# A two-layer decoder on one core: the opening of the chained gated MLP in another engine order

## The chip, the core and the metric

The kernel runs on one core of one Trainium2 chip. The metric is the device time of one execution in microseconds (us), and lower is better. The kernel before takes 1467.89 us, the median of 3 runs (1467.75 to 1471.22).

The engines are named as the profile names them: PE is the matrix engine (PEld its weight loads), DVE the vector engine, ACT the scalar engine, POOL the general engine, which here only issues accumulating transfers, and SP the engine that issues the loads. Each engine takes its instructions in the order of its queue.

## The reference

Two layers over 512 tokens of width 1024, all in float32. Each layer is a token mixer, a cross-attention into 256 memory tokens, and a gated MLP; what concerns the change is the end of the attention and the MLP:

```
def cross_attn(x, mem, norm, mem_norm, wq, wk, wv, wo):
    ...
    s = jnp.einsum('bqhd,bkhd->bhqk', q, k).astype(jnp.float32) * (XA_HD ** -0.5)
    p = jax.nn.softmax(s, axis=-1).astype(x.dtype)
    o = jnp.einsum('bhqk,bkhd->bqhd', p, v).reshape(Bn, S, D_MODEL)
    return o @ wo

def conv_ffn(x, norm, w_up, dw_w, dw_b, w_down):
    h = rms_norm(x, norm) @ w_up
    g = causal_dwconv(h[..., :D_FF], dw_w, dw_b)
    u = h[..., D_FF:]
    return (jax.nn.gelu(g) * u) @ w_down

def reference(...):
    for layer in range(DEPTH):
        ...
        x = x + cross_attn(x, mem, ...)
        x = x + conv_ffn(x, f_norm[layer], f_w_up[layer], ...)
    return rms_norm(x, final_norm)
```

D_FF is 3072, so the MLP has 24 chunks of 128 channels on the gate side and 24 on the value side; the convolution has width 3 and runs along the tokens.

## The kernel before

**Number format.** Every float32 operand of a product is split in two: `high` copies it with ACT into the matrix format, `low` subtracts that copy from the original with DVE. A product of 128 x 128 by 128 x 512 is then three matmuls (`mm3`, L184: high by high, high by low, low by high). So each weight piece costs a load (SP), an ACT copy, a DVE subtraction and PE time.

**The MLP's units.** The first two of the 24 chunks (PLAIN = 2) are computed plainly, in `opening` (L991): four products of 24 matmuls each, `start(0)` to `start(3)` (gate 0, value 0, gate 1, value 1), with weight pieces called w0 to w3 here, each loaded into one of three `raw` buffers. The other 22 chunks are computed in pairs of gate and value by a scheme of seven block products instead of eight (`unit`, L925): the weight pair of a chunk is held as four blocks, and sums of blocks are needed too. The two input sums of the scheme are made by `Seven.sums` (L742) from the token activations, four calls, the last of them in the opening.

**The blocks of a weight pair** (`Blocks`, L777). `load` brings two blocks into a `raw` buffer (r and z), `load_second` brings a12 and a22 into two of four `wa` buffers. The sums are made in place by accumulating transfers that POOL issues, one after the other, inside `low`: after a11 is split, r += z; after a22, z += a22; after s3, r += a22; after s2, r += a12. So the blocks a11, s3, s2, s4 are the same buffer r at four times, s1 is z after its transfer, and `high("s3")` has to wait until r += z has landed. `wa` buffers become free when s3 (a22) and s2 (a12) are done.

The first pair, chunk 2, is called the first pair below (`first` in the code, `up` in the attention), chunk 3 the second (`second`).

**The order.** In the units of the attention and in the whole MLP the order of PE, ACT, DVE and POOL is the program's (`tc.manual_schedule(engines=ORDERED)`); SP's loads are ordered by a planner at build time. The end of the attention (L695 to L724) is not written out: there the planner orders all engines from its own estimates of durations, in which a piece that is traced earlier has priority among those that it takes to be ready. This end consists of the output products `back(n, ks)` (24 matmuls for each of eight n), the scores and softmax of the last head (`scores(3)`: PE, then DVE L501 to L505, the exponentials on ACT L510, DVE L515, the scaling on ACT L517), its transposes on PE (L531), the split of these (`turned(3)`), its product with the values (`mixed(3)`), the splits of the first pair's blocks a11, a22, a12, s3 and s1 (`prepare`), and three of the four calls of `sums`.

**The opening before.** PE runs start(0), the mean of squares for the norm (L287, L288), start(1), start(2), start(3), then a11 of the first pair (`ahead`, L918). ACT copies that result into a second bank (L922); after that PE can add s2 to the second bank, having done s1 in a third. ACT and DVE meanwhile make the root and the reciprocal of the norm (L306, L308), the splits of w2 and w3, the gate chains of chunks 0 and 1 (L1008 scale, L889 first tap, L892 two more taps, L894 gelu, L1011), the products with the values (L1014, L1016, L1019), the fourth `sums`, and the splits s2 of the first pair and a11 and a22 of the second. L922 is traced last of all of these on ACT.

ACT holds one set of function tables at a time; a load of another set shows as ACT_TABLE_LOAD before the first function that needs it. Copies, squares and the linear taps run with whichever set is there.

Of the kernel before, what the change touches and what calls it, by code (L numbers as in the profile page):

```python
# [10 lines left out]
F32 = mybir.dt.float32  # L11
F32R = mybir.dt.float32r
AF = mybir.ActivationFunctionType
# [48 lines left out]
def trunk(ctx: ExitStack, tc: tile.TileContext, I: dict, out: list):  # L62
# [407 lines left out]
    def attention(layer, norm, mem, nxt, six, up):  # L470
# [17 lines left out]
        def score(h, half):  # L488
            ps = aux_ps()
            for j in range(2):  # L490
                qc = 2 * half + j
                for d in range(2):
                    c = 2 * h + d
                    mm3(
                        ps[:, j * M : (j + 1) * M], blk(q[c], qc * P),
                        mem.key(c), d == 0, d == 1,
                    )
            mx = small.tile([P, 2], F32, tag="mx", name=nm("mx"))
            e = tmp_f()
            both = e.rearrange("p (a b) -> p a b", a=2)  # L500
            V.tensor_tensor(  # L501
                both, ps.rearrange("p (a b) -> p a b", a=2), Memory.r.unsqueeze(1).broadcast_to([P, 2, M]), op=ALU.mult
            )
            V.tensor_reduce(mx, both, axis=mybir.AxisListType.X, op=ALU.max)
            V.tensor_tensor(mx, mx, rq[:, 2 * half : 2 * half + 2], op=ALU.mult)  # L505
            yield
            sm = small.tile([P, 2], F32, tag="sm", name=nm("sm"))
            for j in range(2):
                qc = 4 + 2 * half + j
                A.activation(  # L510
                    e[:, j * M : (j + 1) * M], e[:, j * M : (j + 1) * M], AF.Exp,
                    bias=mx[:, j : j + 1], scale=rq[:, qc : qc + 1], accum_out=sm[:, j : j + 1],
                )
            yield
            V.reciprocal(sm, sm)  # L515
            for j in range(2):
                A.activation(e[:, j * M : (j + 1) * M], e[:, j * M : (j + 1) * M], AF.Copy, scale=sm[:, j : j + 1])  # L517
            es.setdefault(h, []).append(e)
            yield

        def scores(h):
            for half in range(2):
                for _ in score(h, half):
                    pass
# [20 lines left out]
        def mixed(h):  # L545
            for d, out in enumerate(mix(h)):
                o[2 * h + d] = split(out)
# [154 lines left out]

        back(0, range(4))
        mixed(2)
        scores(3)
        back(0, range(4, 6))
        back(4, range(6))
        prepare("a11")
        transpose(3)
        turned(3)  # L710
        back(1, range(6))
        prepare("a22")
        mixed(3)
        prepare("a12", "s3")
        seven = Seven(nxt)
        for k in range(4):
            for n in (k, k + 4):
                back(n, range(6 if n in acc else 0, C))
            if k == 1:
                prepare("s1")  # L720
            if k < 3:
                for _ in seven.sums(k):
                    pass
# [53 lines left out]
    class Blocks:  # L777
# [8 lines left out]
            self.r, self.z = raw[:, :T], raw[:, T:]  # L786

        def load_second(self):
            self.a12, self.a22 = [tmp.tile([P, T + 4], F32, tag="h", name=nm("wa"), bufs=4)[:, :T] for _ in range(2)]
            nc.sync.dma_start(self.a12, self.src[:, D + T :])  # L790
            nc.sync.dma_start(self.a22, self.src[:, D : D + T])

        def high(self, name):
            if self.ring:
# [38 lines left out]
    def ffn(layer, norm, nxt, seven, pairs):  # L833
# [91 lines left out]
        def unit(c):  # L925

            nonlocal left, chains
            G, F = chains
            down, seeded = downs.get(c), c > GC
            H = main_ps()[:, :M]  # L930
            m(c, H, "s1", seven.T1)
            high(c + 1, "s3")
            next(left, None)
            low(c + 1, "s3")

            m(c, F, "s2", seven.T2, False)
            next(left, None)
            u, f, g = tmp_f(), tmp_f(), tmp_f()
            A.activation(u[:, :M], F, AF.Copy)
            next(left, None)  # L940
            high(c + 1, "a22")

            m(c, G, "a12", seven.B21, False)
            next(left, None)
            if down:
                d = [down.bank(i, seeded) for i in range(2)]
            next(left, None)
            low(c + 1, "a22")
            times_r(g, G, left_half)
            high(c, "s4")  # L950

            m(c, F, "s3", seven.T3, False)
            A.activation(u[:, M:], F, AF.Copy)
            low(c, "s4")
            add(f[:, right_half], H, u[:, M:])
            V.tensor_tensor(f[:, right_half], f[:, right_half], norm.r[:, right_half], op=ALU.mult)
            high(c + 2, "a11")
            low(c + 2, "a11")
            high(c + 1, "a12")
            low(c + 1, "a12")  # L960
            if down:
                for ks in (range(GC - 1), (GC - 1,)):
                    for i in range(2):
                        down.products(i, d[i], seeded, ks)
            if c + 3 in pairs:
                pairs[c + 3].load()
            if c + 2 in pairs:
                pairs[c + 2].load_second()
            if c >= GC - 1 and c + 1 in downs:
                downs[c + 1].w.high()  # L970
                downs[c + 1].w.low()
            if c + 2 in downs and c + 2 <= CF:
                downs[c + 2].load()
            high(c + 1, "s1")
            low(c + 1, "s1")
            high(c + 1, "s2")
            low(c + 1, "s2")
            if down:
                down.home(0, d[0], seeded)

            if c + 1 in pairs:
                chains = ahead(c + 1)
            if down:
                down.home(1, d[1], seeded)

            m(c, H, "s4", seven.B22, False)
            m(c, F, "a22", seven.T4, False)
            left = gating(c, g, f, u, F, H)
            next(left)

        def opening():  # L991

            nonlocal left, chains
            ps, y = {}, {}

            def start(i):
                ps[i] = main_ps()
                x = w.pop(0)
                for k in range(C):
                    mm3(ps[i], blk(x, k * P), norm.x[k], k == 0, k == C - 1)  # L1000

            def fetch(i):
                w.append(Piece(I["wup"][(layer * 2 + i % 2) * PLAIN + i // 2]))
                w[-1].high()

            def gate(c):
                g = tmp_f()
                V.tensor_tensor(g, ps.pop(2 * c), norm.r, op=ALU.mult)  # L1008
                for y[c] in gate_conv(c, g):
                    yield  # L1010
                V.tensor_tensor(y[c], y[c], norm.r, op=ALU.mult)  # L1011

            def values(c):
                V.tensor_tensor(y[c], ps.pop(2 * c + 1), y[c], op=ALU.mult)  # L1014
                ys[c] = act_r(), act_r()
                A.activation(ys[c][0], y[c], AF.Copy)  # L1016

            def close(c):
                V.tensor_tensor(ys[c][1], y[c], ys[c][0].bitcast(F32), op=ALU.subtract)  # L1019

            def both(c, name):
                high(c, name)
                low(c, name)

            ss = split(norm.ss)
            start(0)
            fetch(2)
            w[-1].low()
            norm.r = scale_of(mean_of(ss))
            Norm.due = None  # L1030

            start(1)
            fetch(3)
            w[-1].low()
            g = gate(0)
            next(g)
            both(first, "s2")
            next(g)
            next(g)
            pairs[second].load()  # L1040
            pairs[second].load_second()
            downs[GC].load()
            t = seven.sums(3)
            next(t)
            next(g, None)

            start(2)
            next(t, None)
            values(0)
            both(second, "a11")  # L1050
            close(0)

            start(3)
            g = gate(1)
            next(g)
            both(second, "a22")
            next(g)
            next(g)
            pairs[second + 1].load()
            next(g, None)  # L1060
            chains = ahead(first)

            def rest():
                values(1)
                yield
                close(1)

            left = rest()

        left, chains = None, None  # L1070
        first, second = PLAIN, PLAIN + 1
        done.update((first, name) for name in ("a11", "a22", "a12", "s3", "s1"))
        with tc.high_priority(AHEAD):
            w = [Piece(I["wup"][(layer * 2 + k) * PLAIN]) for k in range(2)]
            for x in w:
# [803 lines left out]
```

## Time and profile before

| | |
|---|---|
| median of 3 runs | 1467.89 us (1467.75 to 1471.22) |
| profiled execution, its own time | 1468.71 us |
| its span, first to last instruction | 1466.9 us |
| granted PE clock, mean of the span | 0.989 |
| PEld, DVE, ACT, POOL busy | 87%, 74%, 62%, 22% of the span |

The profile is one execution. A row of a timeline gives the start, the duration, the engine, the line of the kernel, the operation, output<-inputs with the shape, the count of merged instructions, and in brackets the idle time before it with what released it. Matmuls overlap: at full clock a 128x512 matmul is listed with 0.39 us but starts 0.23 us after the one before, and a 128x256 one with 0.28 us starts 0.12 us after. Time on PE is therefore best read from start to start. The two layers are two separate passes through the code: layer 0's attention ends and its MLP opens between about 300 and 420 us, layer 1's between about 1005 and 1125 us.

### The profile page before, as it was taken

The page shows a single profiled execution, that of the slowest core. Times are in us where ns is not written, and L with a number is a line of the kernel's source. Part 1 is how long each engine was busy: PE and PEld are TensorE (multiplying, and loading weights), DVE is VectorE, ACT ScalarE, POOL GpSimd, SP SyncE. Part 2 cuts the span into 40 slices and gives each one's busy share as a digit, 9 for nine tenths or more (in the row PEclk, how much of TensorE's full clock was granted, in tenths as well). Part 3 has the DMA queues.
Part 4 walks back from the last instruction along what each step waited for, and adds up shares of the span by engine and source line. Part 5 has one row for each costly group of instructions (what it writes and reads, how often), then busy time and mean ns, then how long its engine had stood idle before and what let it go on. Part 6 is the DMA issues. An engine that isn't in the chain of part 4 may idle for free.

```text
span 1466.9 us, 22867 instructions
## 1 busy us (share of the span) xinstructions
PE 1430.8 (98%) x8650; PEld 1270.4 (87%) x8650; DVE 1079.3 (74%) x1796; ACT 905.0 (62%) x1588; POOL 317.7 (22%) x333
## 2 busy tenths in 40 slices
PE   9999999999899999999999999998989999999998
PEld 7988888978799999999988777897868999999997
DVE  6987775858677666676789997877767676676665
ACT  7678755657456666566665558676555565666664
POOL 0012300200122222222008991011002222222211
PEclk9999999999999999999999999999999999999999
DMA  8522333543477777677442364255237777777651
GB/s 294 192 86 87 98 117 80 118 106 101 112 172 189 163 166 181 161 166 173 130 129 86 116 181 150 79 113 122 89 94 164 172 167 183 164 174 178 154 135 58
DMA packets 80319, 205.37 MB, mean 140 GB/s; under 512 B 9040, under 2 KB 9552, under 8 KB 80208
## 3 DMA queue, kind: packets, MB, share of 16 engines
q1 hardware_dynamic: 51120, 151.20, 33.6%
q0 software_dynamic: 28800, 52.44, 20.3%
q8 instruction: 67, 1.10, 0.3%
q14 instruction: 44, 0.36, 0.1%
q10 hardware_dynamic: 288, 0.27, 0.1%
HBM read 146.21 MB, written 2.10 MB: 101 GB/s over the span
## 4 chain that ended last, share of the span: by engine, by line
PE 81%; DVE 6%; DMA 5%; ACT 3%; issue 3%; POOL 2%; SPq 0%; POOLq 0%; ACTq 0%; DVEq 0%
PE mm L186 19%; PE mm L187 19%; PE mm L188 19%; PE aux L186 7%; PE aux L187 7%; PE aux L188 7%; PE mm L458 2%; DMA raw<-wa 2%; DMA raw<-raw 1%; DMA raw<-in_wv 1%; DVE bigr L817 1%; POOL actf L1480 1%; ACT tmp L510 1%; DVE tmp L892 1%; DVE wlo L167 0%
## 5 line engine op out<-in xcount | busy, mean ns | idle before, releaser
L187 PE MATMUL mm<-act,whi 128*128 128x512 f32 (+2 forms) x1061 | 370.7, 349 | 0.5 <-DVE act L181 0.4
L186 PE MATMUL mm<-act,whi 128*128 128x512 f32 (+2 forms) x1061 | 370.7, 350 | 0.0
L188 PE MATMUL mm<-act,wlo 128*128 128x512 f32 (+2 forms) x1061 | 370.3, 349 | 0.0
L187 PEld LDWEIGHTS mm<-act,whi 128*128 128x128 f32 x1061 | 201.9, 190 | 27.8 <-DVE act L167 1.0
L186 PEld LDWEIGHTS mm<-act,whi 128*128 128x128 f32 x1061 | 202.0, 191 | 27.6 <-ACT tmp L1479 0.8
L188 PEld LDWEIGHTS mm<-act,wlo 128*128 128x128 f32 x1061 | 201.8, 190 | 25.3 <-DVE wlo L167 0.6
L186 PE MATMUL mm<-bigr,bigr 128*128 128x256 f32 x704 | 202.0, 287 | 16.4 <-ACT mm L922 11.9
L188 PE MATMUL mm<-bigr,bigr 128*128 128x256 f32 x704 | 201.1, 286 | 0.4 <-DVE bigr L817 0.4
L187 PE MATMUL mm<-bigr,bigr 128*128 128x256 f32 x704 | 200.9, 285 | 0.0
L810 ACT ACTIVATE bigr<-raw 128x512 fp32r<-128x512 f32 x176 | 105.4, 621 | 109.1 <-DMA raw<-wa 97.2
L817 DVE TENSOR_TENSOR bigr<-raw,bigr 128x512 fp32r<-128x512 f32 x176 | 117.6, 688 | 70.5 <-ACT bigr L810 70.5
L186 PE MATMUL aux<-act,whi 128*128 128x512 f32 x399 | 155.9, 391 | 0.0
L187 PE MATMUL aux<-act,whi 128*128 128x512 f32 x399 | 155.7, 390 | 0.0
L188 PE MATMUL aux<-act,wlo 128*128 128x512 f32 x399 | 155.2, 389 | 0.0
L186 PEld LDWEIGHTS mm<-bigr,bigr 128*128 128x128 f32 x704 | 136.8, 194 | 18.0 <-ACT mm L922 12.3
L166 ACT ACTIVATE whi<-raw 128x1024 fp32r<-128x1024 f32 (+1 forms) x95 | 96.5, 1020 | 85.8 <-PE mm L187 46.2
L188 PEld LDWEIGHTS mm<-bigr,bigr 128*128 128x128 f32 x704 | 136.9, 194 | 0.9 <-DVE bigr L817 0.9
L187 PEld LDWEIGHTS mm<-bigr,bigr 128*128 128x128 f32 x704 | 137.0, 195 | 0.0
L820 POOL DMA_DIRECT2D raw<-raw x50 | 43.2, 864 | 329.9 <-DVE wlo L817 193.0
L828 POOL DMA_DIRECT2D raw<-wa x50 | 43.1, 862 | 299.6 <-DVE bigr L817 211.7
L167 DVE TENSOR_TENSOR wlo<-raw,whi 128x1024 fp32r<-128x1024 f32 (+1 forms) x75 | 90.3, 1209 | 22.3 <-ACT whi L166 22.0
L171 DVE TENSOR_TENSOR tmp<-mm,tmp 128x256 f32<-128x256 f32 x130 | 53.9, 419 | 65.8 <-PE mm L188 64.1
(353 smaller groups left out, 3126.4 us busy)
## 6 DMA issues: line engine op xcount, KB each, us to landing
raw<-wa POOLq DMA_DIRECT2D x150, 256.0 KB, 5.3
wa<-in_wpair SPq DMA_DIRECT2D x88, 256.0 KB, 3.3
raw<-in_wpair SPq DMA_DIRECT2D x44, 512.0 KB, 4.8
big<-in_wdown SPq DMA_DIRECT2D x44, 512.0 KB, 4.2
raw<-raw POOLq DMA_DIRECT2D x50, 256.0 KB, 4.8
raw<-in_pw SPq DMA_DIRECT2D x24, 512.0 KB, 3.3
raw<-in_win SPq DMA_DIRECT2D x20, 512.0 KB, 3.3
raw<-in_wk SPq DMA_DIRECT2D x16, 512.0 KB, 3.7
```

The lines of the kernel that those rows point to most:

```text
L166: A.activation(hi, src, AF.Copy)
L167: fetched[1] = (eng or V).tensor_tensor(lo, src, hi.bitcast(F32), op=ALU.subtract)
L171: V.tensor_tensor(out, a, b, op=ALU.add)
L186: PE.matmul(ps, wh, xh, start=first, stop=False, skip_group_check=onto)
L187: PE.matmul(ps, wh, xl, start=False, stop=False, skip_group_check=onto)
L188: PE.matmul(ps, wl, xh, start=False, stop=last, skip_group_check=onto)
L458: PE.matmul(p, m[j], x, start=k == 0 and j == 0 and x is hi, stop=k == C - 1 and x is lo)
L510: A.activation(e[:, j * M : (j + 1) * M], e[:, j * M : (j + 1) * M], AF.Exp, bias=mx[:, j : j + 1], scale=rq[:, qc : qc + 1], accum_out=sm ...
L810: A.activation(self.w[name][0], self.block(name), AF.Copy)
L817: V.tensor_tensor(lo, self.block(name), hi.bitcast(F32), op=ALU.subtract)
L820: G.dma_start(self.r, self.z, accum_op=ALU.add)
L828: G.dma_start(self.r, self.a12, accum_op=ALU.add)
```

## The change

In the attention's last head:

```diff
             for j in range(2):
-                A.activation(e[:, j * M : (j + 1) * M], e[:, j * M : (j + 1) * M], AF.Copy, scale=sm[:, j : j + 1])
+                part = e[:, j * M : (j + 1) * M]
+                score.last = A.activation(part, part, AF.Copy, scale=sm[:, j : j + 1]).ins
...
         mixed(2)
+        prepare("a11", "a22")
         scores(3)
         back(0, range(4, 6))
         back(4, range(6))
-        prepare("a11")
         transpose(3)
         turned(3)
         back(1, range(6))
-        prepare("a22")
+        with tc.issue_after(score.last):
+            A.activation(small.tile([P, 1], F32, tag="warm", name=nm("root"), bufs=1), eps, AF.Sqrt)
+            prepare("a12", "s3")
         mixed(3)
-        prepare("a12", "s3")
...
-            if k == 1:
-                prepare("s1")
+            if k in (1, 2):
+                prepare("s%d" % k)
```

`issue_after` queues ACT's instructions of the block behind the last scaling of the softmax, in order of issue only. The tiny square root makes the table load happen there. s2 of the first pair is now split here, at k = 2, and no longer in the opening.

In the loads of a pair, a22 comes before a12; in the first unit the load of the pair after next moves to the opening:

```diff
-            self.a12, self.a22 = [...]
-            nc.sync.dma_start(self.a12, self.src[:, D + T :])
+            self.a22, self.a12 = [...]
             nc.sync.dma_start(self.a22, self.src[:, D : D + T])
+            nc.sync.dma_start(self.a12, self.src[:, D + T :])
...
-            if c + 2 in pairs:
+            if c + 2 in pairs and c > first:
                 pairs[c + 2].load_second()
```

In the opening:

```diff
-            norm.r = scale_of(mean_of(ss))
+            start(1, range(1))
+            mean = mean_of(ss)
             Norm.due = None
-
-            start(1)
+            root = tmp_f()
+            A.activation(root, mean, AF.Sqrt, bias=eps)
+            A.activation(small.tile([P, 1], F32, tag="warm", name=nm("gelu"), bufs=1), eps, AF.Gelu_apprx_tanh)
+            norm.r = small.tile([P, T], F32, tag="r", name=nm("r"), bufs=1)
+            V.reciprocal(norm.r, root)
+            start(1, range(1, C))
+            pairs[second].load()
+            pairs[second].load_second()
             fetch(3)
-            w[-1].low()
             g = gate(0)
             next(g)
-            both(first, "s2")
-            next(g)
-            next(g)
-            pairs[second].load()
-            pairs[second].load_second()
+            w[-1].low()
+            pairs[second + 1].load()
+            pairs[second + 1].load_second()
             downs[GC].load()
-            t = seven.sums(3)
+            t = seven.sums(3, lambda: (next(g), next(g)))
             next(t)
             next(g, None)
 
             start(2)
+            both(second, "a11")
+            values(0)
             next(t, None)
-            values(0)
-            both(second, "a11")
             close(0)
...
             next(g)
             next(g)
-            pairs[second + 1].load()
             next(g, None)
             chains = ahead(first)
...
-        done.update((first, name) for name in ("a11", "a22", "a12", "s3", "s1"))
+        done.update((first, name) for name in ("a11", "a22", "a12", "s3", "s1", "s2"))
```

`start(i, ks)` now takes the range of the eight contraction steps, so the first step of start(1), three matmuls, runs before the mean. The function handed to `sums` is called between its two ACT copies (L747) and its DVE differences (L753 to L759): the second and third tap of gate 0 and its gelu come there.

More of the change, by code (lines that the diff above doesn't have):

```diff
@@ L788, in load_second @@
         def load_second(self):
-            self.a12, self.a22 = [tmp.tile([P, T + 4], F32, tag="h", name=nm("wa"), bufs=4)[:, :T] for _ in range(2)]
+            self.a22, self.a12 = [tmp.tile([P, T + 4], F32, tag="h", name=nm("wa"), bufs=4)[:, :T] for _ in range(2)]
+            nc.sync.dma_start(self.a22, self.src[:, D : D + T])
             nc.sync.dma_start(self.a12, self.src[:, D + T :])
-            nc.sync.dma_start(self.a22, self.src[:, D : D + T])
         def high(self, name):
@@ L994, in opening, with start @@
             ps, y = {}, {}
[L996 to L1000, printed above, removed]
+            def start(i, ks=range(C)):
+                if ks[0] == 0:
+                    ps[i] = main_ps()
+                for k in ks:
+                    mm3(ps[i], blk(w[0], k * P), norm.x[k], k == 0, k == C - 1)
+                if ks[-1] == C - 1:
+                    w.pop(0)
             def fetch(i):
```

## The prediction

> **What bounds the kernel now.** I read the busy times on the page first, then PE's waits, then PE's timeline around each long wait, then the queues of the engine that ended it.
>
> ```profile
> PE 1430.8 (98%) x8650; PEld 1270.4 (87%) x8650; DVE 1079.3 (74%) x1796; ACT 905.0 (62%) x1588; POOL 317.7 (22%) x333
> ...
> PE mm L186 <- ACT mm L922: 11.9, 2, 6.0
> PE aux L531 <- ACT tmp L517: 7.0, 4, 2.9
> PE mm L186 <- ACT bigr L810: 3.0, 2, 1.6
> ```
>
> PE is the bound, so only its holes are worth anything. The change aims at the two largest rows: the copy L922 in the two MLP openings and the softmax of the last head (L517) in the two attention ends. The third stays (below).
>
> The softmax hole, layer 0 and then layer 1, from start to start:
>
> ```profile
> 302.25 1.03 PE L531 MATMUL aux<-ident,tmp 128*128 128x128 f32 x8
> 303.04 0.48 PE L186 MATMUL mm<-act,whi 128*128 128x512 f32 x1
> ...
> 316.69 0.39 PE L188 MATMUL mm<-act,wlo 128*128 128x512 f32 x1
> ...
> 321.04 1.54 PE L531 MATMUL aux<-ident,tmp 128*128 128x128 f32 x6 [0.85 <-ACT tmp L517]
> 322.24 0.78 PE L186 MATMUL mm<-act,whi 128*128 128x512 f32 x1
> 322.81 0.63 PE L187 MATMUL mm<-act,whi 128*128 128x512 f32 x1
> ...
> 326.17 0.40 PE L186 MATMUL mm<-act,whi 128*128 128x512 f32 x1
> ...
> 1021.43 0.39 PE L188 MATMUL mm<-act,wlo 128*128 128x512 f32 x1
> ...
> 1029.38 0.39 PE L187 MATMUL mm<-act,whi 128*128 128x512 f32 x1
> ```
>
> The first two rows give eight transposes at full clock: 0.79 us. From 316.69 to 326.17 are 9.48 us for one 0.23 step, eight transposes and nine 0.23 steps, which need 0.23 + 0.79 + 2.04 = 3.06. So layer 0 loses 6.4 us: the wait itself, and then 0.63 us matmuls at a lower clock. In layer 1, 7.95 us hold one step, eight transposes and four steps (1.93): 6.0 lost.
>
> Why the softmax is late:
>
> ```profile
> 310.86 0.68 DVE L501 TENSOR_TENSOR tmp<-aux,rs 128x512 f32<-128x512 f32 x1
> 315.02 0.69 DVE L817 TENSOR_TENSOR bigr<-raw,bigr 128x512 fp32r<-128x512 f32 x1 [3.48 <-ACT bigr L810]
> 315.63 0.68 DVE L504 TENSOR_REDUCE mx<-tmp 128x2 f32<-128x512 f32 x1
> ...
> 314.35 0.63 ACT L810 ACTIVATE bigr<-raw 128x512 fp32r<-128x512 f32 x1 [4.98 <-DMA raw<-raw]
> ```
>
> The split of s3 stands in both queues in the middle of the softmax and waits for r += z to land. DVE idles 3.48 us for it with the maximum (L504) queued behind.
>
> The openings, layer 0, then layer 1 with its mean:
>
> ```profile
> 386.13 0.28 PE L188 MATMUL mm<-act,wlo 128*128 128x256 f32 x1
> 386.78 0.38 PE L186 MATMUL mm<-bigr,bigr 128*128 128x256 f32 x1 [0.37 <-DVE tmp L1014]
> ...
> 388.19 0.28 PE L188 MATMUL mm<-bigr,bigr 128*128 128x256 f32 x1
> 394.43 0.58 PE L186 MATMUL mm<-bigr,bigr 128*128 128x256 f32 x1 [5.96 <-ACT mm L922]
> ...
> 397.80 0.28 PE L186 MATMUL mm<-act,whi 128*128 128x256 f32 x1
> ...
> 1072.13 0.39 PE L188 MATMUL mm<-act,wlo 128*128 128x512 f32 x1
> 1073.58 0.50 PE L288 MATMUL stat<-act,ones 128*128 128x512 f32 x1 [0.23 <-DVE act L167]
> 1073.92 0.39 PE L186 MATMUL mm<-act,whi 128*128 128x512 f32 x1
> ...
> 1091.59 0.28 PE L188 MATMUL mm<-act,wlo 128*128 128x256 f32 x1
> 1104.45 0.28 PE L186 MATMUL mm<-act,whi 128*128 128x256 f32 x1
> ```
>
> Layer 0: 386.13 to 397.80 is 11.67 us for 28 starts (1 + 11 + 1 + 15), which need 28 x 0.12 = 3.36; lost 8.3. Layer 1: 12.86 us for 34 starts (1 + 11 + 1 + 21; 4.08); lost 8.8. The mean in layer 1: 1.79 us for three 0.23 steps; lost 1.1, because its input comes late. All holes together: 6.4 + 6.0 + 8.3 + 8.8 + 1.1 = 30.6 us. That is the ceiling of this change.
>
> **The change part by part.**
>
> *Softmax.* a12 and s3 go behind the last scaling on ACT, and so behind the softmax on DVE too, since their subtraction needs ACT's copy. L504 then follows L501 at 310.86 + 0.60 = 311.5 instead of 315.63, 4.2 earlier, and the third transpose, which needs the second half, is released at 321.04 - 4.2 = 316.9. PE is free at 316.69 + 0.23 = 316.9. The hole closes, and the lower clock with it: 12.4 us for both layers. s3 loses nothing by coming later: r += z landed at 314.35, before its new turn, and its first reader on PE is in the units, 70 us on.
>
> *New in that place*: a table load and a tiny root on ACT, ahead of `turned(3)`.
>
> ```profile
> 894.00 0.60 ACT L1626 ACTIVATE tmp<-aux 128x512 f32<-128x512 f32 x1 [1.12 <-PE aux L298]
> 894.62 1.28 ACT L1627 ACT_TABLE_LOAD   x1
> 895.91 0.20 ACT L1627 ACTIVATE root<-tmp 128x1 f32<-128x1 f32 x1
> ```
>
> Such a pair took 1.5 us elsewhere. Behind it wait the two copies of `turned(3)`, their subtractions, and `mixed(3)` on PE; ahead of `mixed(3)` PE has `back(1)`, 18 steps of 0.23 = 4.1 us, and the copies and subtractions need some 2 of them (0.63 and 0.69 a piece, as in the rows above, partly side by side). So I cost it at nothing; without that cover it is 1.5 per layer. The Trainium skill (ScalarE: Activation LUTs, What ACT_TABLE_LOAD costs) counts a drain of about 1.38 us besides the 1.28, 2.66 per switch. The rows above show no such gap: the load begins 0.02 us after a busy ACT ends and the next function starts 0.01 us after it. By the page each hold in the tail would be 2.9 us, still about inside the cover, and the two loads that leave the opening's chain would free 5.3 instead of 2.6 us; the sum on PE would hardly move, since PE's holes are the ceiling.
>
> *Opening.* L922 is the end of a chain; here are its parts that change:
>
> ```profile
> 368.72 1.28 ACT L306 ACT_TABLE_LOAD   x1 [0.72 <-PE stat L288]
> 370.02 0.69 ACT L306 ACTIVATE tmp<-stat,eps 128x512 f32<-128x512 f32 x1
> ...
> 374.01 1.16 DVE L203 TENSOR_TENSOR wlo<-raw,whi 128x1024 fp32r<-128x1024 f32 x1
> 375.08 0.68 DVE L1008 TENSOR_TENSOR tmp<-mm,r 128x512 f32<-128x512 f32 x1
> ...
> 377.84 0.75 DVE L892 SCALAR_TENSOR_TENSOR tmp<-tmp,par,tmp 128x511 f32<-128x511 f32 x1
> ...
> 382.63 0.42 DVE L753 TENSOR_TENSOR tmp<-tmp,tmp 128x256 f32<-128x256 f32 x1 [3.26 <-ACT tmp L747]
> ...
> 387.95 0.69 DVE L817 TENSOR_TENSOR wlo<-raw,whi 128x512 fp32r<-128x512 f32 x1 [1.22 <-ACT whi L810]
> ```
>
> (a) The root's table is loaded before: 1.30, but three matmuls of start(1) come ahead of the mean, 0.68 later in layer 0: 0.6 gained. In layer 1 the mean's input is late anyway, so the full 1.3. (b) w3's subtraction no longer stands between reciprocal and L1008: 1.07. (c) L1008 to the taps: 2.76 before, with s2's split between; after, L1008 (0.61) and w3's subtraction (1.14): 1.0 gained. (d) DVE's 3.26 us behind gelu's table load and ACT's two copies go, since the load is done during the reciprocal and the copies during w3's subtraction: 3.3. (e) DVE's 1.22 for a11's copy shrinks to about 0.7, as that copy is queued ahead of L1016: 0.5. Sum: 6.5 in layer 0, 7.2 in layer 1.
>
> What is needed: in layer 0 the hole before 394.43 (6.12 beyond a step) and the one before 386.78 (0.53), 6.65; in layer 1 the same and the mean's 1.11, 7.75. So 0.2 and 0.6 us stay. Holes this short should not lower the clock as 6 us did. What is late next is still L922, with no slack.
>
> *Moved loads.* The second pair's raw load goes ahead of w3's, so w3 gets the buffer that w2 frees:
>
> ```profile
> 345.77 14.21 SPq L195 DMA_DIRECT2D raw<-in_wup  x4
> 369.29 6.24 SPq L785 DMA_DIRECT2D raw<-in_wpair  x2
> ...
> raw<-in_wup SPq DMA_DIRECT2D x4, 512.0 KB, 3.3
> ```
>
> w3 was issued by 360.0 and will be at 369.3, where the second pair's was; with 3.3 us it lands at 372.6, its copy (twice as wide as the 0.63 one above, so about 1.1) ends at 373.7, and L889, queued behind on ACT, has its input about 374.0 (L1008 at 375.08 - 0.6 - 1.07, and 0.6 for itself). Covered by a third of a us. start(3) needs w3 only after start(1) and start(2), 48 steps of 0.23 or 11 us after the mean. a22 before a12, and both earlier, cost nothing: PE has waited on neither. s2's split in the tail adds 0.5 on ACT and 0.6 on DVE at k = 2; start(0)'s 5.4 us and the three moved matmuls hide it; uncovered, up to 0.6 per layer.
>
> *What stays.* The third row of PE's waits, 3.0 us in two, is the stall at s1 of chunk 4. It hangs on POOL's transfers, which start from the first unit's progress; they move with PE, and the units are unchanged.
>
> **Sum.** 30.6 - 0.2 - 0.6 = 29.8. For what the trace of before can't show (the planner's new order in the attention's end, the root's load) I take 1.3 off, between 0 and 3.0 + 1.2 (both covers gone): 28.5. From the profiled execution's 1468.7 that gives 1440.2; the median lies 0.8 below that execution: 1439.4 us.
>
> **The rivals.**
> - *A new wait for w3* (15%). If w3's load takes longer, ACT's copy of it holds back L889 and the whole chain. The cover is thin, and a load at that place shares the DMA engines with the second pair's. Landing 3 us later, plus about 1.5 of low clock as after 394.43, costs 4 per layer: 1447.
> - *The softmax hole stays in part* (10%), because the planner puts another waiting split into the softmax, or s3's ahead of `turned(3)`. For it: it did so before. Against: r += z lands early enough. Half of 12.4 lost: 1446; all: 1452.
> - *The gain is given back at chunk 4* (8%): POOL's transfers take their own time while PE comes 8 us earlier. Against: they start behind L953 of the same unit. 4 per layer: 1447.
> - *Better* (7%): the stall at chunk 4 goes as well (3.0): 1436.
> - *It doesn't do what it says* (2%): the planner's order and L922 stay: 1467.
> - *Slower* (2%): w3's load stands on SP's in-order queue behind a `wa` load that waits for the first pair's s3 or s2. Each us late beyond the cover is paid on both layers; it decides against the change at (28.5 + 4.4) / 2 = 16.5 us. No load here took half of that; 1475.
>
> My forecast has 56%. The range 1435 to 1451 takes it, the better case and nearly all of the first three rivals. About 0.3% (4.4 us) is what a measurement of this kernel can tell from no change: faster 0.95, same 0.03, slower 0.02.
>
> **What would show it.** PE's waits on L922 under 1.5 us in total and on L517 under 1; no 0.63 us matmuls after the last transposes; no table load between the mean and the reciprocal; the wait on s1 (L810) still near 3 us. Wrong would be a wait of ACT on w3's load ahead of L889, or a longer row of PE on L810.

## The result and the profile after

The kernel after takes 1446.2 us, the median of 4 runs (1444.8 to 1447.83), beside 1467.91 us for the kernel before in the same call (4 runs, 1467.75 to 1471.22): a ratio of 0.9847, 95% interval 0.983 to 0.9864, or 21.7 us less. The forecast was 1439.4 us, range 1435 to 1451. The profiled execution of after is its slowest, 1447.83 us (span 1446.0), 20.9 us under the profiled execution of before; the ledger below is made between these two.

First the busy times on the page and the longest of PE's waits (us in total, times, longest):

```profile
PE 1424.8 (99%) x8650; PEld 1264.9 (87%) x8650; DVE 1079.0 (75%) x1796; ACT 906.1 (63%) x1592; POOL 318.2 (22%) x333
...
PE mm L186 <- ACT bigr L812: 4.0, 2, 2.0
PE stat L298 <- DVE actf L1502: 1.7, 1, 1.7
PE mm L186 <- DVE tmp L171: 1.3, 2, 0.7
PE mm L186 <- ACT tmp L941: 1.1, 2, 0.8
PE mm L186 <- ACT whi L801: 1.1, 2, 0.6
PE mm L186 <- ACT mm L924: 1.1, 2, 0.6
```

Lines have moved by one or two: L922 is now L924, L810 is L812, L517 is L518. The copy's wait fell from 11.9 to 1.1 us and the softmax's 7.0 us are gone. But the stall at s1 grew from 3.0 to 4.0, L171 from 0.4 to 1.3, and L801, the weight copies of the last attention unit, is new. L298 lies between the two layers, outside the stretches that the change touches; it was 0.9 in before.

The same stretches of PE as in the prediction, from start to start. The softmax of layer 0 and of layer 1:

```profile
317.92 0.39 PE L188 MATMUL mm<-act,wlo 128*128 128x512 f32 x1
318.15 1.03 PE L532 MATMUL aux<-ident,tmp 128*128 128x128 f32 x8
...
321.08 0.39 PE L186 MATMUL mm<-act,whi 128*128 128x512 f32 x1
...
1012.12 0.39 PE L188 MATMUL mm<-act,wlo 128*128 128x512 f32 x1
1012.35 1.03 PE L532 MATMUL aux<-ident,tmp 128*128 128x128 f32 x8
...
1014.15 0.39 PE L187 MATMUL mm<-act,whi 128*128 128x512 f32 x1
```

The eight transposes stand in one row again, with no idle time and no 0.63 us matmuls behind them. Layer 0 takes 321.08 - 317.92 = 3.16 us where it took 9.48; layer 1 takes 2.03 where it took 7.95.

The openings, then the stall at s1 that ends the first units:

```profile
381.04 0.28 PE L188 MATMUL mm<-act,wlo 128*128 128x256 f32 x1
...
383.32 0.39 PE L186 MATMUL mm<-bigr,bigr 128*128 128x256 f32 x1 [0.56 <-ACT mm L924]
...
385.22 0.28 PE L186 MATMUL mm<-act,whi 128*128 128x256 f32 x1
...
405.79 0.39 PE L186 MATMUL mm<-bigr,bigr 128*128 128x256 f32 x1 [1.94 <-ACT bigr L812]
...
1056.42 0.40 PE L186 MATMUL mm<-act,whi 128*128 128x512 f32 x1
1057.09 0.50 PE L187 MATMUL mm<-act,whi 128*128 128x512 f32 x1 [0.26 <-DVE act L223]
...
1059.14 0.50 PE L288 MATMUL stat<-act,ones 128*128 128x512 f32 x1 [0.22 <-DVE act L167]
1059.48 0.40 PE L186 MATMUL mm<-act,whi 128*128 128x512 f32 x1
...
1076.45 0.28 PE L188 MATMUL mm<-act,wlo 128*128 128x256 f32 x1
...
1078.72 0.39 PE L186 MATMUL mm<-bigr,bigr 128*128 128x256 f32 x1 [0.55 <-ACT mm L924]
...
1081.34 0.28 PE L186 MATMUL mm<-act,whi 128*128 128x256 f32 x1
...
1101.64 0.39 PE L186 MATMUL mm<-bigr,bigr 128*128 128x256 f32 x1 [2.02 <-ACT bigr L812]
```

And the two s1 stalls of before, which the prediction had not shown:

```profile
416.93 0.39 PE L186 MATMUL mm<-bigr,bigr 128*128 128x256 f32 x1 [1.59 <-ACT bigr L810]
...
1122.72 0.39 PE L186 MATMUL mm<-bigr,bigr 128*128 128x256 f32 x1 [1.45 <-ACT bigr L810]
```

PE runs the same 8650 matmuls in nearly the same order, so the two traces can be matched matmul by matmul, and the difference of the starts is what has been gained so far:

| stretch | forecast | measured |
|---|---|---|
| last attention unit, layer 0 / 1 | 0 | -1.4 / -1.1 |
| softmax | +6.4 / +6.0 | +6.3 / +5.9 |
| mean, layer 1 | +1.1 | -0.1 |
| opening, less what was to stay of L922 | +8.1 / +8.2 | +7.5 / +8.0 |
| end of opening to the stall at s1 | 0 | -1.4 / -2.0 |
| all the rest | -1.3 | -0.8 |
| sum | 28.5 | 20.9 |

The openings are 11.67 - (385.22 - 381.04) = 7.5 and 12.86 - (1081.34 - 1076.45) = 8.0. The stretch to s1 took 416.93 - 397.80 = 19.13 us in layer 0 and takes 405.79 - 385.22 = 20.57; in layer 1 it took 1122.72 - 1104.45 = 18.27 and takes 20.30. So the holes that the change aims at closed nearly as forecast. 7.6 us are missing: 2.5 in the last attention unit and 3.4 in the first units, both costed at nothing, 1.2 in the mean, and 1.0 in the sizes of the holes, less the 0.5 by which the allowance was too large. (Layer 1 also loses 1.4 in the last attention unit, and has 0.3 of it back before the softmax.) "All the rest" is the sum of larger amounts: 0.8 lost at L298, where of the ten kernels tried below nine wait 0.6 to 0.8 us and one 1.8, so that it says nothing of the change; and 1.5 lost right behind the s1 of layer 1, where PE's granted clock is 0.50 over 1103.5 to 1106.8 us in after and was 1.00 in before, of which 1.1 comes back later in the units.

**The last attention unit.** ACT in layer 0, after:

```profile
280.66 0.63 ACT L812 ACTIVATE bigr<-wa 128x512 fp32r<-128x512 f32 x1 [3.62 <-DMA wa<-in_wpair]
281.20 0.59 ACT L510 ACTIVATE tmp<-tmp,mx,rq 128x256 f32<-128x256 f32 x1
```

and before:

```profile
279.65 0.60 ACT L510 ACTIVATE tmp<-tmp,mx,rq 128x256 f32<-128x256 f32 x1 [2.44 <-DVE mx L505]
...
286.58 0.63 ACT L810 ACTIVATE bigr<-wa 128x512 fp32r<-128x512 f32 x1 [0.80 <-DMA wa<-in_wpair]
```

Block a22 of the first pair is now traced ahead of `scores(3)` and loaded first, and the planner puts its split ahead of a softmax's exponentials, where ACT waits 3.62 us for the load. It is the same fault as the one that the change removes from the last head, one unit earlier.

### The profile page after: what moved, and what is told of

Read it like the earlier page. It is cut to its first block, busy times and chain, and to the rows that moved or that the text cites. A ratio compares the mean times of both kernels' runs of the same rounds, so it can differ in the third digit from the quotient of the medians.

```text
span 1446.0 us, 22842 instructions
## 1 busy us (share of the span) xinstructions
PE 1424.8 (99%) x8650; PEld 1264.9 (87%) x8650; DVE 1079.0 (75%) x1796; ACT 906.1 (63%) x1592; POOL 318.2 (22%) x333
## 4 chain that ended last, share of the span: by engine, by line
PE 80%; issue 7%; DMA 5%; DVE 4%; ACT 2%; POOL 2%; SPq 0%; POOLq 0%; ACTq 0%; DVEq 0%
PE mm L188 19%; PE mm L187 19%; PE mm L186 19%; PE aux L186 7%; PE aux L187 7%; PE aux L188 7%; DMA raw<-wa 1%; PE mm L458 1%; DMA raw<-raw 1%; DMA raw<-in_wv 1%; DVE wlo L167 1%; POOL actf L1487 1%; ACT whi L166 1%; POOL act L167 0%; DMA wa<-in_wpair 0%
## 5 line engine op out<-in xcount | busy, mean ns | idle before, releaser
L812 ACT ACTIVATE bigr<-raw 128x512 fp32r<-128x512 f32 x176 | 105.2, 621 | 81.1 <-DMA raw<-wa 76.2
L166 ACT ACTIVATE whi<-raw 128x1024 fp32r<-128x1024 f32 (+1 forms) x95 | 96.5, 1020 | 87.1 <-PE mm L187 46.4
L171 DVE TENSOR_TENSOR tmp<-mm,tmp 128x256 f32<-128x256 f32 x130 | 53.9, 419 | 86.3 <-PE mm L188 84.6
L167 DVE TENSOR_TENSOR wlo<-raw,whi 128x1024 fp32r<-128x1024 f32 (+1 forms) x75 | 90.3, 1210 | 22.0 <-ACT whi L166 21.7
```

Of the source, the lines that this page charges most:

```text
L166: A.activation(hi, src, AF.Copy)
L167: fetched[1] = (eng or V).tensor_tensor(lo, src, hi.bitcast(F32), op=ALU.subtract)
L171: V.tensor_tensor(out, a, b, op=ALU.add)
L812: A.activation(self.w[name][0], self.block(name), AF.Copy)
```

## The experiments

Each was timed in three rounds beside the kernel before, whose medians were 1469.48, 1469.8 and 1469.57 us in the three calls. Ratios are to the kernel before, each with its 95% interval; "after" has 0.9847 (0.983 to 0.9864). After was timed in another call, in which before had 1467.91 us, so a difference from after below is one between medians of two calls; by the ratios the kernel tried comes out up to 1.7 us lower. Differences of 2 us or less therefore rest on the traces, where PE's time for one stretch can be compared from start to start.

### The softmax part, alone and undone

Alone, in the kernel before, without the root's load and without any other part:

```diff
-                A.activation(e[...], e[...], AF.Copy, scale=...)
+                score.last = A.activation(..., AF.Copy, scale=...).ins
...
-        prepare("a12", "s3")
+        with tc.issue_after(score.last):
+            prepare("a12", "s3")
```

> The kernel before with one edit: a12 and s3 of the first pair are queued behind the last scaling of the softmax; no early table, no new opening, old order of loads. Theory (the two parts of the gain are independent): the softmax hole closes in both layers, 6.4 + 6.0 us, so 1455.5 us, with PE's wait on L517 near 0 and the wait of 11.9 us on L922 unchanged. Rival (the opening is bound by the transfers and loads, so PE that comes earlier only waits longer there): the wait on L922 grows by what the softmax gives, and the time stays within 4 us of 1467.9.

1456.2 us (1455.78 to 1457.12), ratio 0.9913 (0.9899 to 0.9928): 13.3 us gained. PE's waits hold no L518 any more and the copy's row as it was:

```profile
PE mm L186 <- ACT mm L924: 11.9, 2, 5.9
PE mm L186 <- ACT bigr L812: 3.8, 2, 2.1
```

Undone, in the kernel after:

```diff
         with tc.issue_after(score.last):
             A.activation(small.tile([P, 1], F32, tag="warm", ...), eps, AF.Sqrt)
-            prepare("a12", "s3")
         mixed(3)
+        prepare("a12", "s3")
```

> The changed kernel with a12 and s3 no longer queued behind the softmax (the table load stays there). Theory: the planner puts s3's split into the softmax again, PE waits on the scaling as before and its clock falls: 12.4 us more than the changed kernel, 1458.6 us. Rival (the earlier priority of a11 and the loads of a22 first brought the gain, not the queueing): within 3 us of 1446.2.

1459.4 us (1458.52 to 1461.29), ratio 0.9936 (0.9919 to 0.9952): 13.2 us lost against after, and the wait is there again:

```profile
PE aux L532 <- ACT tmp L518: 8.0, 4, 3.0
```

Both ways the term is 13 us, against 12.4 forecast. The two parts of the change add up: 0.87% for the softmax part alone and 0.64% for all the rest without it make 1.51%, where both together took off 1.53%.

### The early tables

The kernel after without the tiny root and the tiny gelu:

```diff
-            A.activation(small.tile([P, 1], ..., name=nm("root"), ...), eps, AF.Sqrt)
...
-            A.activation(small.tile([P, 1], ..., name=nm("gelu"), ...), eps, AF.Gelu_apprx_tanh)
```

> The changed kernel without the two tiny functions that load the tables early, so that the loads come before the root and before gelu again. Theory: the root's load puts 1.3 us into the chain, gelu's another 1.3 less what DVE has to do meanwhile; the chain has no slack, so PE's wait on L924 grows by 2.0 to 2.6 us per layer, and a window at half clock may come back (1.7 us each): 1450 to 1454 us. Rival (the new engine order alone covers the loads): within 1 us of 1446.2.

1451.01 us (1450.09 to 1452.91), ratio 0.9873 (0.9858 to 0.9887): 4.8 us lost.

```profile
PE mm L186 <- ACT mm L923: 5.0, 2, 2.5
```

PE's wait on the copy grows from 1.1 to 5.0 us; the two early loads are worth nearly all that they take out of the chain, 2.6 per layer less what slack was there. Without them the opening of layer 0 still falls from 11.67 to 6.12 us, so the larger part of its gain comes from the new order of the engines. How this part is shared among the steps of that order, (b) to (e) in the forecast, no run shows.

### w3's load ahead of the second pair's

```diff
+            fetch(3)
             pairs[second].load()
             pairs[second].load_second()
-            fetch(3)
```

> The changed kernel with w3's load ahead of the second pair's again. Theory: in the changed kernel ACT waits 2.0 us for w3 and gate 0's chain is 0.3 to 0.4 us late; with w3 loaded 10 us earlier PE's wait on L924 (0.56 and 0.55 us) falls to about 0.2 each, and the time to about 1445.5 us. Rival (the chain is not bound by w3 but by DVE's own length): the wait on L924 stays at 0.5 and the time within 0.5 us of the changed kernel's.

1446.0 us (1445.64 to 1448.11), ratio 0.984 (0.9824 to 0.9857): the time of after. The wait on the copy is gone altogether, but another has grown:

```profile
PE mm L186 <- ACT tmp L941: 3.5, 3, 2.2
```

This is the chain that the forecast's first rival named. In after, ACT waits for w3 with the first tap queued behind:

```profile
368.50 1.06 ACT L200 ACTIVATE whi<-raw 128x1024 fp32r<-128x1024 f32 x1 [1.97 <-DMA raw<-in_wup]
369.47 0.80 ACT L891 ACTIVATE tmp<-tmp,par 128x512 f32<-128x512 f32 x1
```

Without this wait, L924's goes. But L941, the copy behind chunk 4's r += z, takes 2.4 us more in the units, and so no gain shows in all. Where the wait on L941 comes from is below.

### a22's split where it was

First by the program: `a22` goes back behind the last head's softmax.

```diff
-        prepare("a11", "a22")
+        prepare("a11")
         scores(3)
...
-            prepare("a12", "s3")
+            prepare("a22", "a12", "s3")
```

> The changed kernel with the split of a22 of the first pair behind the softmax too, ahead of a12 and s3, instead of ahead of scores(3). Theory: in the changed kernel the planner put this split into the last unit's softmax in ACT's queue, where it waits 3.6 us for its load, and PE loses 1.2 us (layer 0) and 1.4 us (layer 1) at 283 and 977 us; with the split later both go: 1443.6 us and no PE wait on L801. Rival (a12 of the attention's own pairs comes too late since a22 is loaded first): the waits on L801 stay, 1446.

1444.06 us (1442.5 to 1446.17), ratio 0.9831 (0.9816 to 0.9846). PE has no wait on L801 any more; 2.1 us less than after, against 2.5 in the ledger.

Then by the loads alone, which undoes the third part of the change:

```diff
-            nc.sync.dma_start(self.a22, self.src[:, D : D + T])
             nc.sync.dma_start(self.a12, self.src[:, D + T :])
+            nc.sync.dma_start(self.a22, self.src[:, D : D + T])
```

> The changed kernel with the old order of a pair's second half, a12 before a22: this undoes 'lower right block loaded first' alone. Theory: that order has no use of its own here, and its price is that a22's split is placed inside the last attention unit's softmax, where ACT waits 3.6 us for the load. With a12 first, a22 is issued some 6 us later, the split is placed after the softmax as in the kernel before, PE's waits on L801 (1.1 us) go, and the time is that of the run that put the split last: about 1444 us (1442.5 to 1445.5). Rival 1: the order matters in the units, where z += a22 waits for a22 to land, so the wait on s1 (4.0 us) grows by a us or more and the time is 1447 to 1450. Rival 2: neither, the planner places the split as now: 1446, L801's rows unchanged.

1443.79 us (1442.84 to 1444.43), ratio 0.9819 (0.9796 to 0.9842): 2.4 us less than after. The split stands behind the softmax as in before, and waits little:

```profile
286.02 0.63 ACT L812 ACTIVATE bigr<-wa 128x512 fp32r<-128x512 f32 x1 [0.97 <-DMA wa<-in_wpair]
```

The wait on s1 is 3.8 us there, so the rival's use of the new order in the units did not show at s1. Each of the two intervals overlaps that of after; it is the two together, and the vanished L801 row in both, that carry the reading: the place of a22's split in the new order costs about 2 us. That loading the lower right block first brings nothing is not shown: with a12 first, PE's wait on L941 is 3.3 us where after has 1.1. Kernels with a22 first have up to 4.5 there, so this need not come from the order of the loads.

### Who holds the stall at s1

Chunk 4's r += z, then r += a22 and z += a22 stand in this order on POOL (start of the issue), in after:

```profile
390.14 0.86 POOL L822 DMA_DIRECT2D raw<-raw  x1 [3.87 <-DVE wlo L819]
...
397.10 0.86 POOL L826 DMA_DIRECT2D raw<-wa  x1 [4.30 <-DVE bigr L819]
397.64 1.21 POOL L824 DMA_DIRECT2D raw<-wa  x1
```

z += a22, the last row, makes s1. It needs nothing from s3, but stands on POOL behind s3's r += a22, which waits for s3's split, which waits for r += z. ACT's wait for r += z and then that for s1, in after:

```profile
395.45 0.63 ACT L812 ACTIVATE bigr<-raw 128x512 fp32r<-128x512 f32 x1 [2.16 <-DMA raw<-raw]
...
405.11 1.15 ACT L812 ACTIVATE bigr<-raw 128x512 fp32r<-128x512 f32 x2 [4.07 <-DMA raw<-wa]
```

From the issue of r += z to s3's split are 5.3 us, and from that of z += a22 to s1's split 7.5. The L941 copy is queued behind the first of these rows, s1's matmuls wait for the second. Chunk 4's r += z itself is slower than it was. In before, layer 0: the 512 KB load of the next pair (SP), then r += z (POOL), and its time from issue to landing:

```profile
400.27 0.43 SPq L785 DMA_DIRECT2D raw<-in_wpair  x1
...
402.71 0.86 POOL L820 DMA_DIRECT2D raw<-raw  x1 [5.33 <-DVE wlo L817]
...
raw<-raw POOLq DMA_DIRECT2D x1, 256.0 KB, 3.9
```

And in after, where r += z is the row at 390.14 above:

```profile
389.17 0.42 SPq L787 DMA_DIRECT2D raw<-in_wpair  x1
...
raw<-raw POOLq DMA_DIRECT2D x1, 256.0 KB, 5.2
```

The load used to be issued 2.4 us ahead of r += z and is now issued 1.0 ahead, so that both are in flight together for longer. The same two numbers in every kernel where r += z of chunk 4 stands in the first unit, with PE's wait on L941 in the second unit (us, layer 0 / layer 1):

| kernel | load issued ahead of r += z by | r += z takes | PE waits on L941 |
|---|---|---|---|
| softmax_only | 2.6 / 2.7 | 4.0 / 3.7 | 0 / 0 |
| before | 2.4 / 2.7 | 3.9 / 3.3 | 0 / 0 |
| z_first (below) | 1.0 / -0.1 | 5.1 / 6.5 | 0.28 / 1.82 |
| no_tables | 1.0 / -0.1 | 5.2 / 6.4 | 0.38 / 1.68 |
| after | 1.0 / 0.5 | 5.2 / 5.4 | 0.39 / 0.76 |
| softmax_back | 0.6 / 0.1 | 5.3 / 6.2 | 0.49 / 1.52 |
| a22_late | 1.0 / 0.5 | 5.4 / 5.4 | 0.56 / 0.72 |
| w3_first | 1.0 / 0.3 | 5.7 / 6.9 | 0.83 / 2.25 |
| loads_late (below) | 1.0 / 0.0 | 6.0 / 6.9 | 1.17 / 2.20 |
| a12_first | 1.0 / 0.0 | 6.1 / 6.3 | 1.23 / 1.62 |

To within rounding, PE's wait on L941 is the time of r += z less 4.8 us in layer 0 and less 4.7 in layer 1, and nothing where r += z takes less. So the transfer's time sets this wait. The r += z before it, which has no load beside it in after, takes 3.3 us. That the load beside it is what slows chunk 4's fits the rows: with a lead of 2.4 us or more it takes 4.0 at most, with 1.0 or less 5.1 at least. But no run moves that load alone.

Three kernels go further. The first moves a11 of chunk 4 into the opening, so that r += z starts earlier:

```diff
             both(second, "a22")
+            high(second + 1, "a11")
             next(g)
+            low(second + 1, "a11")
             next(g)
```

> The changed kernel with the split of a11 of chunk 4, and so POOL's r += z of chunk 4, in the opening, where ACT and DVE have a hole behind gate 1's first tap, instead of late in the first unit. Theory: the stalls in the second unit and at s1 of chunk 4 (L941 0.4 and 0.8, L171 0.7 and 0.7, s1 1.9 and 2.0 us, and one window of 3.4 us at half clock each, 1.7 us) come from r += z of chunk 4 landing late, with the two transfers behind it; they go: about 8 us less, 1438 us, and no half-clock window at 407 and 1103 us. Rival (z += a22 is slow by itself beside the other transfers, and POOL issues it only behind s3's): the wait on s1 stays near 2 us in each layer, and 1 to 2 us at most are gained, 1445 us.

1442.58 us (1440.82 to 1442.68), ratio 0.9817 (0.9802 to 0.9832): 3.6 us less than after. The waits on L941 in the second unit and on L171 are gone; the stall at s1 stays, and the time is 4.6 us above the 1438 expected. Its row of PE's waits:

```profile
PE mm L186 <- ACT bigr L812: 3.7, 2, 2.0
```

and of its POOL rows chunk 4's r += z and z += a22:

```profile
382.99 0.86 POOL L822 DMA_DIRECT2D raw<-raw  x1 [2.85 <-DVE wlo L819]
...
395.51 1.21 POOL L824 DMA_DIRECT2D raw<-wa  x1
```

r += z starts 7.2 us earlier than in after (390.14), z += a22 only 2.1 (397.64): s3's transfer still stands ahead of it, and a22 of this pair is loaded no sooner. Of the theory the half on L941 and L171 holds; on s1 the rival was right.

The second puts z += a22 ahead of s3's transfer on POOL, at the end of the unit before:

```diff
+        def sum_z(self):
+            if not self.summed:
+                G.dma_start(self.z, self.a22, accum_op=ALU.add)
+            self.summed = True
...
             high(c + 1, "s2")
             low(c + 1, "s2")
+            if c + 2 in pairs:
+                pairs[c + 2].sum_z()
```

> The changed kernel with POOL's z += a22 of the pair after next issued at the end of a unit, ahead of that pair's r += a22 (s3), instead of behind it; nothing else moved. Theory (s1 of chunk 4 is late because z += a22 stands behind s3's transfer on POOL, which waits for ACT's and DVE's split of s3, and then shares the engines with it): it starts 2 us earlier and alone, the wait on s1 (1.9 and 2.0 us) falls under 0.5, and the half-clock windows at 407 and 1103 us go: 3 to 7 us less, about 1441 us. Rival (r += z is what is late, and POOL's order does not matter): the wait on s1 keeps over 1.5 us and the time stays within 1.5 us of 1446.2.

1442.42 us (1441.06 to 1442.88), ratio 0.9811 (0.9796 to 0.9826): 3.8 us less than after. No row of PE names s1 any more; part of it comes back at L941:

```profile
PE mm L186 <- ACT tmp L946: 4.7, 4, 1.8
```

Of these 4.7 us, 2.1 are the two waits in the table above; the other two, 1.3 each, come one unit later and are new. So the order on POOL holds s1. The third asks whether the loads of chunk 4's pair, which the change moved into the opening, slow its transfers:

```diff
-            pairs[second + 1].load()
-            pairs[second + 1].load_second()
             downs[GC].load()
...
+            pairs[second + 1].load()
             next(g, None)
...
-            if c + 2 in pairs and c > first:
+            if c + 2 in pairs:
                 pairs[c + 2].load_second()
```

> The changed kernel with the loads of chunk 4's pair where they were before: its first half after the taps of gate 1, its second half in the first unit. Theory (the first unit starts sooner while POOL's transfers take their time): the wait on s1 stays at 3.5 to 4.5 us and the time within 1.5 us of 1446. Rival 1 (the moved loads run beside r += z of chunk 4 and slow it from 3.9 to 5.3 us): that transfer comes back under 4.5 us, the waits on L941 and L171 (2.4 us together) shrink by half or more, and the time is about 1444. Rival 2 (a22 now lands too late for z += a22): the wait on s1 grows beyond 5 us and the time is 1448 or more.

1447.4 us (1446.55 to 1448.94), ratio 0.9847 (0.9827 to 0.9867): no change, and the wait on s1 is 3.4 us. But the trial is weaker than meant. a22 of chunk 4 is loaded at the same place of the first unit in both, since SP can only issue it when s3 of the first pair frees its buffer:

```profile
387.91 0.33 SPq L792 DMA_DIRECT2D wa<-in_wpair  x1
388.29 0.42 SPq L787 DMA_DIRECT2D raw<-in_wpair  x1
```

In after the same two are issued at 388.79 and 389.17, and everything around them is 0.9 us later as well. So the place of these lines in the program has no effect, but the rival's cause, that loads beside r += z slow it, was not tried by this; the table above is what the record has on it.

### All of it together

`a22_late`, `w3_first`, `a11_early` and `z_first` in one kernel:

> The changed kernel with four edits together: a22's split of the first pair behind the softmax, w3 loaded first, a11 of chunk 4 split in the opening, z += a22 ahead of r += a22 on POOL. Theory: no wait on L801, none over 0.3 on L924, none on L171 or L941 in the second unit, and s1 of chunk 4 there in time: 1446.2 - 2.1 - 0.8 - 8 = 1435 us, with no half-clock window between 300 and 1130 us. Rival (s1 is bound by the time of the transfer): 1441 us with the wait on s1 near 2 us per layer.

1435.43 us (1433.19 to 1437.49), ratio 0.9765 (0.975 to 0.9779): 10.8 us under after and 34.4 under before, faster than both. The four alone gained 2.1, 0.2, 3.6 and 3.8, 9.7 together. Of the waits that this document speaks of, one is left above half a us in the MLP:

```profile
PE mm L186 <- ACT tmp L946: 1.5, 2, 0.9
```

## Why the prediction was right, and where it was not

Direction, order of size and the mechanism of the gain came as forecast: 21.7 of 28.5 us, inside the range, 6.8 us above the forecast. That the time lies in the range is owed to the room left for the rivals, three of which gave 1446 or 1447, and not to the sum. Both of the forecast's signs of being wrong appeared: ACT waits for w3's load ahead of the first tap (1.97 us in layer 0), and the row at s1 grew from 3.0 to 4.0. Of the terms that failed, two were costed at nothing and one hole was counted as filled. Step by step:

- **Softmax, 6.4 and 6.0.** Right: 6.3 and 5.9 in the trace, and 13 us when done alone or undone alone. The root's table load behind the softmax made no hole on PE, as costed.
- **Opening, 8.1 and 8.2 net.** The right chain, 0.8 too large in all. Taking the tables out of the chain is worth 4.8 us by the run without them. The rival "a new wait for w3" is there, but at 1.1 us of PE's time instead of 8, and removing it alone gained nothing.
- **The mean, 1.1.** This step failed: "in layer 1 the mean's input is late anyway" was taken for a wait that three matmuls ahead of it would fill. The hole stayed: from 1056.42 to 1059.48 PE spends 3.06 us on eight starts of 0.23, so 1.2 are lost, where before lost 1.1. The mean hangs on a chain whose length did not change: from the last x += mm on DVE (L555, now L556) over the last activations (L222, L223) and their squares (L231, L166, L167) to the L288 matmul are 4.33 us in before (1069.25 to 1073.58), in after (1054.81 to 1059.14) and, to 0.01, in each of the other ten kernels. The three matmuls fill their 0.7 us, but PE came 0.8 us sooner against this chain: it began the last step of start(0) 2.43 us behind that x += mm in before and begins it 1.61 behind in after. So PE now waits 0.44 in that step already, on L223, and again on the squares. The new s2 split in this tail is not needed for the loss: softmax_only, where s2 is split in the opening, loses 1.6 at the same place (1058.96 to 1061.65 for five starts).
- **"a22 before a12, and both earlier, cost nothing: PE has waited on neither."** This step failed, with 2.5 us in the trace and 2.1 and 2.4 in the two runs that undo it. That PE did not wait on a block in the old order says nothing about where a planner puts its split in the new one. The rival "the planner puts another waiting split into the softmax" named the mechanism, but looked for it in the last head only.
- **"What stays": the stall at chunk 4 "moves with PE".** This step failed. The stretch from the opening's end to s1 became 1.4 and 2.0 us longer. In layer 0 PE's rows there add 0.4 (L941), 0.4 (L171) and 0.35 (s1). The rival "given back at chunk 4" had the cause, transfers that take their own time, with more than twice the size. They do not only take their time: chunk 4's r += z became slower, 5.2 and 5.4 us where it took 3.9 and 3.3, now that it follows the load more closely, and its time beyond 4.8 and 4.7 is PE's wait on L941. The stall at s1 itself is held by POOL's order, z += a22 behind s3's transfer. With the order changed the wait is gone; with r += z started earlier it is not.
- **The allowance of 1.3** for the planner's order was meant for such things, but it was sized by the two covers that the prediction knew of, and the rest came to 0.8 without them.

Open: why r += z takes 5.1 us in one kernel and 6.1 in another with the load issued 1.0 ahead of it in both, and why the last x += mm is later against PE than it was.

## What to carry to other kernels

Where a planner orders a stretch, a load or a split that is traced earlier can land in another chain's queue and wait there for its data, so after such a change the queues of ACT and DVE are to be read for new waits on DMA, not only in the place that was edited. When holes ahead of a chain of transfers close, the chain becomes the next bound: count the transfers' own time from their issue, with the loads that will be in flight beside them in the new order, and look at what stands ahead of each on its issuing queue, before costing what lies behind at nothing. Work moved ahead of a late input fills the wait only if the engine does not come to that place sooner by as much.

## What was not expected of the hardware

Some stalls of 2 us were followed by half clock on PE, others of the same length were not. The stretch around s1 of layer 0 in after, by engine (stretch, us, PE, PEld, DVE, ACT and POOL busy with their instructions, granted PE clock, DMA share, GB/s), and then the same in loads_late, after a stall of 1.96 us:

```profile
404.00:412.00 8.00, 5.99 (x35) 5.79 (x36) 5.18 (x9) 4.39 (x9) 1.69 (x3) 0.79 0.73 170
```

```profile
404.00:412.00 8.00, 5.58 (x42) 5.17 (x43) 5.18 (x9) 4.45 (x9) 1.75 (x3) 1.00 0.69 167
```

A mean of 0.79 over 8 us is 3.4 us at half clock; over 407.10 to 410.30 alone the granted clock is 0.50. It follows PE's waits of 1.94 and 0.22 us, and costs about 1.4 more: the 15 starts from 407.10 to 410.30 take 3.20 us where they need 15 x 0.12 = 1.80.

```profile
407.10 0.41 PE L186 MATMUL mm<-bigr,bigr 128*128 128x256 f32 x1
...
410.30 0.37 PE L186 MATMUL mm<-bigr,bigr 128*128 128x256 f32 x1
```

The second stretch has none of this, nor has the opening of the kernel without the early tables after its longer stalls of 2.50 and 2.52 us (granted clock 1.00 over 380 to 392 and over 1077 to 1089 us). Of the 20 stalls at s1 in the ten kernels that have them, 1.43 to 2.09 us long, twelve were followed by a stretch at half clock (a granted clock of 0.72 over the 6 us from their end) and eight were not (1.00). The Trainium skill (TensorE: Matmul & The Clock Gate, Why this matters for your kernels) asks for no idle gaps above about 3 us between bursts of matmuls. Here gaps of about 2 us were enough in some places and gaps of 2.5 were not in others; what decides between them no run here shows. For a forecast it means that a stall of 2 us may cost 2 or 3.4, and for a comparison of two kernels that about 1.4 us may come or go with each such stall.
